# Turning the keys of a two-layer hybrid encoder: block transposes on VectorE and short-run stores in place of TensorE transposes

## The chip, the cores and the metric

The kernel runs on one core of one Trainium2 chip, as one program. The metric is the device time of that program in microseconds (us). TensorE is PE in the profile, its weight loads PEld, VectorE DVE, ScalarE ACT, GpSimd POOL and SyncE SP.

## The reference, cut to what matters

Two layers, each a mixer and a feed-forward block over 16 meta tokens and 1024 tokens (L = 1040) of width 1024. In the mixer, four heads of 128 run a gated delta rule forwards and backwards over the tokens in chunks:

```python
proj = h @ w_in
qkv, z, b_raw, a_raw, sc_b, sc_c, sc_h = jnp.split(proj, idx, axis=-1)
qkv = jax.nn.silu(depthwise_conv_centred(qkv, conv_qkv_w))
q, k, v = jnp.split(qkv, 3, axis=-1)
q, k = l2norm(q), l2norm(k)              # per head
...
M = jnp.where(strict, jnp.einsum('bnhid,bnhjd->bnhij', kb, k) * decay_mat, 0.0)
u = triangular_solve(M + I, vb); w = triangular_solve(M + I, kb * exp(G))
attn = jnp.einsum('bnhid,bnhjd->bnhij', q, k) * decay_mat
...
S = S * gl_c + jnp.einsum('bhcd,bhce->bhde', kd_c, v_new)   # in the scan over chunks
```

The last line is why the keys are needed twice: with the head's channels on partitions for the products of keys and queries, and with the tokens on partitions for the update of the state S.

## The kernel before, in words

**Layout.** Activations lie transposed, channels on partitions and 1040 tokens along the row. `KTt` (128 x 4 heads x 1040) is the normalised keys, `QT` the queries. The scan works on nine chunks: the 16 meta tokens, then eight of 128.

**Projections.** `dense` multiplies eight 128 x 128 weight tiles, split into a high and a low part, with a row of tokens in chunks of 348, 346 and 346 (in layer 1's z tiles two of 512): 24 matmuls a chunk, lines 174 to 176, into one of three accumulator banks ("acc"). Weights come by SP's queue, are split on ScalarE (line 129) and VectorE (line 130). A chunk is evicted by VectorE, line 325 in most tiles, into a row buffer (`trow`, three of them); then the bank is free. The tiles come in the order keys (4), queries (4), v (4), then z and short-convolution tiles mixed, z first.

**Side work.** After each chunk `dense` takes one entry from each of three lists (`jobs`, `jobs2`, `jobs3`). Entries are, among others, `k_out`, `chunk_p` (products of keys, lines 478 to 490), `chunk_a` (products of keys and queries, line 514; for the meta chunk with a load of "dt", lines 522 and 523), `v_store` (PE transposes of v, lines 736 and 747, the copy "vm", line 740, eviction and stores, 748 and 749), and the steps of `invert` (lines 582 to 622). This is the order in the source only: a list scheduler at build time sets the order of each engine's instructions from their dependencies, their priorities and the buffers that they wait for. On the chip every engine takes its list in order.

**The inversion.** `substitute(0)` and `substitute(1)`, one for each direction, are 31 pairs of VectorE steps each (lines 555 and 557), every pair on the result of the last; behind each come two block transposes of 128 x 1024 (lines 566 and 567), four ScalarE copies (line 569) and the chain of small matmuls of `invert`. `subs["end"]` is the last step issued.

**Keys to tokens.** `k_out(c)`, called for nine chunks from the fourth tile on: four PE transposes, one a head, into the single "a" bank (line 453), one eviction by ScalarE into a buffer "kt" (line 455), one store on ScalarE's queue of whole 2 KB rows into `vkd` in HBM (line 456). The scan reads it from there as K.

**Buffers that are shared.** `t2k` hands out 128 x 512 buffers of one tag, ck2, five in number: kt, the vm copy, r4 and rows of `query_lengths` (lines 645 to 657), dt and the chunks' qk all take from it. The "a" bank is one, banks "b" and "f" are two each. DMAs on POOL's queue are issued one by one by GpSimd.

Of the kernel before, what the change touches and what calls it, by code (L numbers as in the profile page):

```python
# [10 lines left out]
AF = mybir.ActivationFunctionType  # L11
# [7 lines left out]
H = 4  # L19
# [22 lines left out]
def trunk(ctx: ExitStack, tc: tile.TileContext, xT, w_in, w_ba, w_out, w_gu, w_dn,  # L42
          par_d, alog_d, dtb_d, cst_d, eye_d, out):
    nc = tc.nc
# [16 lines left out]
    def t2k(tag):  # L61
        return sb.tile([128, 4, 128], F32, tag="ck2", bufs=5, name=nm(tag))
# [7 lines left out]
    def pa():  # L70
        return bank("a")
# [26 lines left out]
    act = nc.scalar.activation  # L98
# [5 lines left out]
    adma = nc.scalar.dma_start  # L104
# [204 lines left out]
    for l in range(DEPTH):  # L309
# [23 lines left out]
        def trow():  # L333
            return row(Y[1], F32, 3)
# [109 lines left out]
                qdma(bc, rnd[r + h].partition_broadcast(128))  # L444
                tt(out=dst[:, h, :], in0=dst[:, h, :], in1=bc, op=ALU.mult)

        def k_out(c):

            n = 16 if c == 0 else 128
            s0 = 0 if c == 0 else 16 + 128 * (c - 1)  # L450
            ps = pa()
            for h in range(H):
                nc.tensor.transpose(ps[0:n, h * 128:(h + 1) * 128], KTt[:, h, s0:s0 + n], ident)
            kt = t2k("kt")
            act(out=kt[0:n].rearrange("p a b -> p (a b)"), in_=ps[0:n], func=AF.Copy)
            adma(vkd[c, 0:n, 1, :], kt[0:n].rearrange("p a b -> p (a b)"))


        at0 = [sb.tile([16, 4, 16], F32, tag=f"at0{d}", name=nm("at0")) for d in range(2)]
# [62 lines left out]
                adma(dt_[0:n, :, 0:n], dtd[c, d].rearrange("p (h i) -> p h i", h=4)[0:n, :, 0:n])  # L522
                tt(out=at0[d], in0=qk[0:n, :, 0:n], in1=dt_[0:n, :, 0:n], op=ALU.mult)


        B = [slice(32 * b, 32 * b + 32) for b in range(4)]

        tmp0 = []
        subs = {}
# [137 lines left out]
        for pos, i in enumerate(seq):  # L667
            hh = pos % 4
            if pos == 2:
                gate_weights()  # L670
                evp[0] = base - 60000
            t = trow()
            late = pos < (2, 1)[l]
            if l > 0 and pos == 0:
                dense_by_halves(wload(w_in[l, i], KT), x, FULL, to_row_late(t), first_banks)
            else:
                inproj(i, to_row_late(t) if late else to_row(t), pfirst if l == 0 and pos == 1 else None)
            def convolved(hi=None, lo=None, i=i, hh=hh, t=t, late=late):
                if late:
                    after(tt(out=t, in0=t, in1=rstd, op=ALU.mult), lo)  # L680
                dst = (QT if i < 4 else KTt)[:, hh, :]
                conv(t, dst, P_CV + 3 * i, hi)
                if i >= 4:
                    lengths("k", hh, dst, t)

            if l == 0 and pos == 0:
                held = convolved
                continue
            if l == 0 and pos == 1:
                pre[seq[2]] = wload(w_in[l, seq[2]], KT)  # L690
                held(*lastw)
            convolved()
            if pos == 2:
                g, negG, nGb, negE, gl, bkd = gates()
            nxt = seq[pos + 1] if pos < 7 else 8
            if nxt not in pre:
                pre[nxt] = wload(w_in[l, nxt], KT)
            if pos == 3:
                jobs.extend([None, None] + [lambda c=c: k_out(c) for c in range(9)])
                jobs2.extend([None, None, None] + [lambda c=c: chunk_p(c) for c in range(9)])  # L700

        for hh in range(4):
# [48 lines left out]
        ca = [0, 1, 8, 2, 7, 3, 6, 4, 5]  # L751
        for i in range(4):
            t = trow()
            if i == 2:
                jobs2.extend([lambda c=c: chunk_a(c) for c in ca])
            if i == 3:
                jobs3.extend([None] * (2 * l) + invert(0))
            inproj(8 + i, to_row(t))
            v = trow() if i % 2 == 0 else row(Y[1] + "f")
            conv(t, v, P_CV + 3 * (8 + i))  # L760
            act(out=v, in_=v, func=AF.Silu)
            jobs.extend([lambda i=i, v=v, c0=c0: v_store(i, v, c0) for c0 in (0, 1, 5)])
# [885 lines left out]
```

## Time and profile before

| | |
|---|---|
| runs | 2479.17, 2477.48, 2478.83 us; median 2478.83 |
| profiled execution | 2480.41 us, span 2478.6 us |
| granted TensorE clock | 0.999 |
| busy of the span | PE 99%, PEld 91%, DVE 71%, ACT 42%, POOL 7% |
| first and last key transpose (line 453) | 108.0 to 162.9 us (layer 0), 1349.8 to 1406.2 us (layer 1) |
| HBM | 254.52 MB read, 78.86 MB written |

Busy time counts an engine's instructions with overlaps merged. A group's row gives line, engine, operation, output <- input by the program's names, shape and count, then its busy time in us, the mean ns of one instruction, and the idle time ahead of them with what ended it. Since matmuls are pipelined, the mean of one is longer than the distance between two.

### The profile page before, as it was taken

The numbers are of one execution on the slowest core, as the hardware profiler recorded it, in microseconds if no ns is written. First come the engines' busy times: TensorE is split into PE (matmuls) and PEld (weight loads), VectorE is DVE, ScalarE is ACT, GpSimd is POOL, SyncE is SP. The second block draws the span as 40 slices with busy tenths as digits, with TensorE's granted clock in tenths as the row PEclk, the third lists the DMA queues.
The fourth block names the chain that finished last, engine by engine and source line by source line (L and its number), as shares of the span: only waits on it lengthen the run. The fifth ranks groups of instructions, "written<-read, shape, count | busy, mean of one in ns | idle before, by whom it ended". The sixth has DMA issues, their size and how long they took to land. (4 is left out here: it accounts for less than half of the span.)

```text
span 2478.6 us, 44860 instructions
## 1 busy us (share of the span) xinstructions
PE 2454.0 (99%) x17464; PEld 2253.9 (91%) x17464; DVE 1769.4 (71%) x3268; ACT 1053.3 (42%) x1961; POOL 171.1 (7%) x272
## 2 busy tenths in 40 slices
PE   8999999999999999999999999999999999999998
PEld 6999999999999999999999898998988888888887
DVE  5688255769987777797856883457798776777887
ACT  5675222435333333444546752324453333334454
POOL 0250101002000000000001301000110000000000
PEclk9999999999999999999999999999999999999999
DMA  4453155623432222575524532456434322228734
GB/s 133 129 177 102 62 186 168 218 86 110 149 114 96 94 82 82 200 226 164 159 88 131 171 103 70 154 170 222 126 115 147 111 93 82 81 90 271 232 105 131
DMA packets 198685, 336.34 MB, mean 136 GB/s; under 512 B 23572, under 2 KB 88920, under 8 KB 198472
## 3 DMA queue, kind: packets, MB, share of 16 engines
q1 hardware_dynamic: 174184, 295.31, 36.6%
q0 software_dynamic: 8384, 21.29, 2.8%
q10 hardware_dynamic: 15904, 16.87, 2.0%
q8 instruction: 137, 2.24, 0.4%
q14 instruction: 76, 0.62, 0.1%
HBM read 254.52 MB, written 78.86 MB: 135 GB/s over the span
## 5 line engine op out<-in xcount | busy, mean ns | idle before, releaser
L174 PE MATMUL pacc<-a,whi 128*128 128x346 f32 (+1 forms) x752 | 245.7, 330 | 7.8 <-ACT whi L129 6.0
L176 PE MATMUL pacc<-a,wlo 128*128 128x346 f32 (+1 forms) x752 | 243.9, 326 | 0.0
L174 PE MATMUL pacc<-b,whi 128*128 128x346 f32 (+2 forms) x648 | 226.2, 350 | 0.0
L176 PE MATMUL pacc<-b,wlo 128*128 128x346 f32 (+2 forms) x648 | 223.1, 346 | 0.0
L175 PE MATMUL pacc<-a,whi 128*128 128x346 f32 (+1 forms) x646 | 211.5, 328 | 0.0
L129 ACT ACTIVATE whi<-raw 128x512 fp32r<-128x512 f32 x144 | 90.4, 629 | 280.7 <-PE pacc L175 236.6
L175 PE MATMUL pacc<-b,whi 128*128 128x346 f32 (+2 forms) x559 | 193.2, 346 | 0.4 <-DVE b L954 0.4
L174 PEld LDWEIGHTS pacc<-a,whi 128*128 128x128 f32 x752 | 141.8, 189 | 12.1 <-ACT whi L129 6.0
L176 PEld LDWEIGHTS pacc<-a,wlo 128*128 128x128 f32 x752 | 142.2, 189 | 0.9 <-issue 0.4
L130 DVE TENSOR_TENSOR wlo<-raw,whi 128x512 fp32r<-128x512 f32 x144 | 99.0, 688 | 60.1 <-ACT whi L129 59.3
L174 PEld LDWEIGHTS pacc<-b,whi 128*128 128x128 f32 x648 | 121.8, 188 | 9.7 <-issue 1.5
L176 PEld LDWEIGHTS pacc<-b,wlo 128*128 128x128 f32 x648 | 121.9, 188 | 8.9 <-issue 0.8
L175 PEld LDWEIGHTS pacc<-a,whi 128*128 128x128 f32 x646 | 122.3, 189 | 3.4 <-issue 1.9
L1063 ACT ACTIVATE whi<-rw 128x512 fp32r<-128x512 f32 x98 | 61.5, 631 | 137.2 <-DVE rw L1351 43.1
L175 PEld LDWEIGHTS pacc<-b,whi 128*128 128x128 f32 x559 | 105.2, 188 | 8.1 <-issue 0.8
L1063 ACT ACTIVATE b<-rw 128x512 fp32r<-128x512 f32 x65 | 40.6, 631 | 132.9 <-PE pacc L1083 39.0
L1063 ACT ACTIVATE a<-rw 128x512 fp32r<-128x512 f32 x65 | 40.8, 629 | 111.7 <-PE pacc L1083 78.5
L484 POOL DMA_DIRECT2D ptm<-gd x35 | 19.1, 552 | 844.7 <-DVE a L325 733.7
L1064 DVE TENSOR_TENSOR wlo<-rw,whi 128x512 fp32r<-128x512 f32 x98 | 67.0, 685 | 5.6 <-ACT whi L1063 4.9
L325 DVE TENSOR_TENSOR a<-pacc,rstd 128x346 f32<-128x346 f32 (+2 forms) x59 | 32.5, 554 | 45.2 <-PE pacc L176 45.1
L325 DVE TENSOR_TENSOR b<-pacc,rstd 128x346 f32<-128x346 f32 (+1 forms) x63 | 32.1, 511 | 44.4 <-PE pacc L176 44.2
L1518 PE MATMUL pacc<-P,a 128*128 128x260 f32 x196 | 55.4, 283 | 0.0
(1050 smaller groups left out, 8103.8 us busy)
## 6 DMA issues: line engine op xcount, KB each, us to landing
raw<-in_w_in SPq DMA_DIRECT2D x112, 256.0 KB, 2.7
rw<-in_w_gu SPq DMA_DIRECT2D x96, 256.0 KB, 2.7
raw<-in_w_gu SPq DMA_DIRECT2D x96, 256.0 KB, 2.8
rec<-vkd SPq DMA_DIRECT2D x61, 256.0 KB, 3.0
b<-ad SPq DMA_DIRECT2D x55, 260.0 KB, 4.0
a<-ad SPq DMA_DIRECT2D x55, 256.0 KB, 3.6
rw<-in_w_dn SPq DMA_DIRECT2D x68, 192.0 KB, 3.5
ad<-a SPq DMA_DIRECT2D x21, 520.0 KB, 2.9
```

Source lines behind the costliest of these rows:

```text
L129: lastw[0] = act(out=hi, in_=raw[:, 0:kk, :], func=AF.Copy)
L130: lastw[1] = tt(out=lo, in0=raw[:, 0:kk, :], in1=hi.bitcast(F32), op=ALU.subtract)
L174: mm(ps[:, :n], wh, xh[:, n0:n1], start=(k == 0), stop=False)
L175: mm(ps[:, :n], wh, xl[:, n0:n1], start=False, stop=False)
L176: mm(ps[:, :n], wl, xh[:, n0:n1], start=False, stop=(k == K - 1))
L325: tt(out=t[:, n0:n1], in0=ps, in1=rstd[:, n0:n1], op=ALU.mult)
L484: qdma(gr[0:n, :, 0:n], gd[36 * d + 4 * c:36 * d + 4 * c + 4, 0:n].partition_broadcast(n))
L1063: act(out=hi, in_=src, func=AF.Copy)
L1064: tt(out=lo, in0=src, in1=hi.bitcast(F32), op=ALU.subtract)
L1518: r = mm(ps, wl[:, k, :], th[:, c0:c1], start=False, stop=e, skip_group_check=True)
```

## The change

`k_out` goes. In its place VectorE transposes the keys in blocks of 32 x 32: one instruction takes 512 tokens of one head (128 x 512), and within each of the 4 x 16 blocks rows and columns change places, but the blocks stay where they are. Four stores, one for each group of 32 partitions, then put the blocks where they belong in `vkd`: 512 runs of 32 numbers (128 bytes) each. So there are eight such instructions a layer and one for the meta tokens, with 36 stores, all on POOL's queue. They are called from `jobs2` in the v tiles instead of from `jobs` in the key tiles, and every transpose is made to come after `subs["end"]`, which is the end of `substitute(0)` there. `v`, `B` and the rest are as before.

```diff
@@ -444,16 +444,26 @@
                 qdma(bc, rnd[r + h].partition_broadcast(128))
                 tt(out=dst[:, h, :], in0=dst[:, h, :], in1=bc, op=ALU.mult)
 
-        def k_out(c):
-
-            n = 16 if c == 0 else 128
-            s0 = 0 if c == 0 else 16 + 128 * (c - 1)
-            ps = pa()
-            for h in range(H):
-                nc.tensor.transpose(ps[0:n, h * 128:(h + 1) * 128], KTt[:, h, s0:s0 + n], ident)
-            kt = t2k("kt")
-            act(out=kt[0:n].rearrange("p a b -> p (a b)"), in_=ps[0:n], func=AF.Copy)
-            adma(vkd[c, 0:n, 1, :], kt[0:n].rearrange("p a b -> p (a b)"))
+        B = [slice(32 * b, 32 * b + 32) for b in range(4)]
+
+        def to_tokens(src, half, col, q, prev=None):
+
+            s0 = 16 + 512 * half
+            kt = t2k("kt").rearrange("p a b -> p (a b)")
+            after(nc.vector.transpose(out=kt, in_=src[:, s0:s0 + 512]), prev)
+            for a in range(4):
+                q(vkd[1 + 4 * half:5 + 4 * half, :, col[0], col[1] + 32 * a:col[1] + 32 * a + 32].rearrange("c (b i) j -> i (c b) j", i=32),
+                  kt[B[a]].rearrange("i (t j) -> i t j", j=32))
+
+        def k_turn(h, half):
+
+            if half is None:
+                kt = t2k("kt")[:, :, 0:32]
+                after(nc.vector.transpose(out=kt, in_=KTt[:, :, 0:32]), subs["end"])
+                for a in range(4):
+                    qdma(vkd[0, 0:16, 1, :].rearrange("i (h a j) -> a i h j", h=4, a=4)[a], kt[32 * a:32 * a + 16])
+            else:
+                to_tokens(KTt[:, h, :], half, (1, 128 * h), qdma, subs["end"])
 
 
         at0 = [sb.tile([16, 4, 16], F32, tag=f"at0{d}", name=nm("at0")) for d in range(2)]
@@ -523,8 +533,6 @@
                 tt(out=at0[d], in0=qk[0:n, :, 0:n], in1=dt_[0:n, :, 0:n], op=ALU.mult)
 
 
-        B = [slice(32 * b, 32 * b + 32) for b in range(4)]
-
         tmp0 = []
         subs = {}
         Tm = None
@@ -696,7 +704,6 @@
             if nxt not in pre:
                 pre[nxt] = wload(w_in[l, nxt], KT)
             if pos == 3:
-                jobs.extend([None, None] + [lambda c=c: k_out(c) for c in range(9)])
                 jobs2.extend([None, None, None] + [lambda c=c: chunk_p(c) for c in range(9)])
 
         for hh in range(4):
@@ -751,6 +758,9 @@
         ca = [0, 1, 8, 2, 7, 3, 6, 4, 5]
         for i in range(4):
             t = trow()
+            if i == 0:
+                turns = [(0, None)] + [(h, half) for half in range(2) for h in range(H)]
+                jobs2.extend([lambda n=n: [k_turn(*a) for a in turns[2 * n:2 * n + 2]] for n in range(5)] + [None])
             if i == 2:
                 jobs2.extend([lambda c=c: chunk_a(c) for c in ca])
             if i == 3:
```

A line of the changed kernel is 10 higher than before from 480 to 525, 8 higher from 535 to 706 (substitute: 563 and 565; its transposes: 574 and 575; copies of r4: 654), 7 higher in `v_store` (743, 747, 754), and 10 higher behind.

The scheduler's lists move with it. VectorE around the end of `substitute(0)` of layer 0 (the step with 128x31 is its last; `b_182` is its matrix, `x_1487` that of `substitute(1)`, `pacc` an accumulator bank, `b_257` the row of the first z tile). Before:

```order
L557 TENSOR_TENSOR b_182_1478<-b_182_1478,Tm_1479 128x31
L566 STREAM_TRANSPOSE b_182_1478<-b_182_1478 128x32x32
L567 STREAM_TRANSPOSE b_182_1478<-b_182_1478 128x32x32
L555 TENSOR_TENSOR Tm_1479<-x_1486,x_1487 128x31
L602 COPY b_182_1478<-b_182_1478 32x16x32
L603 COPY b_182_1478<-b_182_1478 32x16x32
L325 TENSOR_TENSOR b_257_2245<-pacc_2258,rstd_81 128x348
L740 COPY vm_2187<-pa_2185 16x128
```

The same place in the changed kernel (`b_164` is the matrix, `kt_...` the new transposes' outputs):

```order
L565 TENSOR_TENSOR b_164_1406<-b_164_1406,Tm_1407 128x31
L462 STREAM_TRANSPOSE kt_1511<-b_38_169 128x4x32
L453 STREAM_TRANSPOSE kt_1517<-b_38_169 128x512
L453 STREAM_TRANSPOSE kt_1549<-b_38_169 128x512
L453 STREAM_TRANSPOSE kt_1555<-b_38_169 128x512
L453 STREAM_TRANSPOSE kt_1587<-b_38_169 128x512
L574 STREAM_TRANSPOSE b_164_1406<-b_164_1406 128x32x32
L575 STREAM_TRANSPOSE b_164_1406<-b_164_1406 128x32x32
L563 TENSOR_TENSOR Tm_1407<-x_1414,x_1415 128x31
```

Five transposes of keys have come in ahead of the matrix's own two, and no eviction of the z tile (line 325) follows. It stands on the same engine behind the end of `substitute(1)` (`b_248` is the first z tile's row, `at_40` the result of the meta chunk that needs a dt load):

```order
L533 TENSOR_TENSOR at_40_171<-pb_1808,dt_1816 16x64
L565 TENSOR_TENSOR x_1415<-x_1415,Tm_1407 128x2x30
L563 TENSOR_TENSOR Tm_1407<-x_1414,x_1415 128x31
L565 TENSOR_TENSOR x_1415<-x_1415,Tm_1407 128x31
L574 STREAM_TRANSPOSE b_318_2893<-x_1415 128x32x32
L575 STREAM_TRANSPOSE x_1414<-x_1415 128x32x32
L325 TENSOR_TENSOR b_248_2227<-pacc_2240,rstd_81 128x348
L325 TENSOR_TENSOR b_248_2227<-pacc_2291,rstd_81 128x346
L325 TENSOR_TENSOR b_248_2227<-pacc_2352,rstd_81 128x346
```

All three evictions of that tile have moved behind 31 pairs of steps and two transposes. In between stand the other four transposes of keys, the first vm copy and the two dt products, which were ahead of the end of `substitute(0)` before.

TensorE in layer 0 at the third chunk of the first z tile. Before, the inversion's first matmuls (line 582) and v's transposes (line 747) lie among the chunk's matmuls:

```order
L174 MATMUL pacc_2309<-a_1_72,whi_2246 128x346
L175 MATMUL pacc_2309<-a_2_73,whi_2246 128x346
L176 MATMUL pacc_2309<-a_1_72,wlo_2247 128x346
L582 MATMUL pf_1978<-b_182_1478,P_884 32x32 x32
L582 MATMUL pf_2013<-b_182_1478,P_884 32x32 x32
L747 MATMUL pa_2284<-ident,b_229_1913 128x128 x4
L174 MATMUL pacc_2309<-a_1_72,whi_2246 128x346
L175 MATMUL pacc_2309<-a_2_73,whi_2246 128x346
```

In the changed kernel the whole chain stands in one piece between the last matmul of that tile (`pacc_2352`) and the first of the second z tile (`pacc_2489`); its end and what follows:

```order
L624 MATMUL pf_2522<-b_164_1406,P_876 64x64 x8
L626 MATMUL pf_2523<-P_876,b_164_1406 64x64 x8
L626 MATMUL pf_2575<-P_876,b_164_1406 64x64 x8
L754 MATMUL pa_1750<-ident,b_178_1599 128x128 x4
L754 MATMUL pa_1801<-ident,b_178_1599 128x128 x4
L524 MATMUL pb_1887<-b_37_168,b_38_169 128x128 x4
L524 MATMUL pb_1952<-b_37_168,b_38_169 128x128 x4
L174 MATMUL pacc_2489<-a_1_72,whi_2477 128x348
```

So the small matmuls have moved from among the projections to a single place ahead of the second z tile, and the transposes of the first v tile (line 754, `b_178`) with them. Another such piece, of `turn`, `v_store` and `chunk_a`, stands behind the second z tile. Layer 1 has the same pieces one chunk of 512 later.

## The prediction

> **What bounds the kernel now.** I read the head of the page first.
>
> ```profile
> span 2478.6 us, 44860 instructions
> PE 2454.0 (99%) x17464; PEld 2253.9 (91%) x17464; DVE 1769.4 (71%) x3268; ACT 1053.3 (42%) x1961; POOL 171.1 (7%) x272
> ```
>
> Then the table by stretches of 10 us (start and end, then busy time and instructions of PE, PE's weight loads, VectorE, ScalarE, GpSimd) for the part of layer 0 that the change touches:
>
> ```profile
> 180.00:190.00 10.00, 10.00 (x66) 9.66 (x65) 8.76 (x20) 2.87 (x4) 0.00 (x0) 1.00 0.19 57
> ...
> 200.00:210.00 10.00, 10.00 (x214) 9.52 (x215) 9.53 (x24) 9.43 (x13) 0.00 (x0) 1.00 0.16 57
> 210.00:220.00 10.00, 10.00 (x215) 9.48 (x208) 9.52 (x23) 7.66 (x13) 1.14 (x1) 1.00 0.47 155
> ```
>
> TensorE works without a gap, so any PE time removed is gained and any PE wait is lost in full, and nothing later can give it back. But VectorE (9.53 and 9.52 of 10) has no room between 200 and 220 us: TensorE stays fed only because VectorE's work is well interleaved there. That is the point on which I decide.
>
> **What is removed.** Per layer 36 PE transposes and nine evictions on ScalarE. From the groups of PE and ACT between 100 and 170 us:
>
> ```profile
> L453 PE MATMUL pa<-ident,b 128*128 128x128 f32 x32 | 4.8, 274 | 0.0
> L455 ACT ACTIVATE kt<-pa 128x512 f32<-128x512 f32 x8 | 4.7, 585 | 2.9 <-PE pa L453 2.5 <-ACT ptm L487 0.4
> ```
>
> Transposes overlap, so their busy time, not their count times 274 ns, is the saving: 4.8/32 x 36 = 5.4 us a layer, 10.8 in all. If nothing else happened, the profiled execution of 2480.4 us (its span is 2478.6) would become 2469.6.
>
> **What is added on VectorE.** The trace has no 128x512 block transpose, but has ones of twice the size.
>
> ```profile
> L545 DVE STREAM_TRANSPOSE b<-b x1: 2093/2093/2093, 151.5 to 151.5; 128x1024 f32<-128x1024 f32 x1
> ```
>
> Half of 2.09 is 1.05 us; the meta one, a quarter of that, 0.3. So eight and one are 8.7 us a layer. They are bound to the end of substitute(0), and there the listed order matters more than their length. Before, VectorE ran thus (one row from further ahead, for its length; then from the end of substitute(0) to behind that of substitute(1); columns: start, duration, and in brackets the idle time ahead and what ended it):
>
> ```profile
> 166.48 0.41 DVE L646 COPY r<-pf 128x260 f32<-128x260 f32 x1
> ...
> 197.02 0.19 DVE L557 TENSOR_TENSOR b<-b,Tm 128x31 f32<-128x31 f32 x1
> 197.25 2.08 DVE L566 STREAM_TRANSPOSE b<-b 128x1024 f32<-128x1024 f32 x1
> ...
> 201.08 0.19 DVE L555 TENSOR_TENSOR Tm<-x,x 128x31 f32<-128x31 f32 x1
> ...
> 202.00 0.52 DVE L325 TENSOR_TENSOR b<-pacc,rstd 128x348 f32<-128x348 f32 x1
> ...
> 206.61 0.21 DVE L555 TENSOR_TENSOR Tm<-x,x 128x60 f32<-128x60 f32 x1
> ...
> 207.28 0.52 DVE L325 TENSOR_TENSOR b<-pacc,rstd 128x346 f32<-128x346 f32 x1
> ...
> 215.74 0.51 DVE L325 TENSOR_TENSOR b<-pacc,rstd 128x346 f32<-128x346 f32 x1
> ...
> 217.63 1.24 DVE L557 TENSOR_TENSOR x<-x,Tm 128x252 f32<-128x252 f32 x1
> ...
> 223.92 0.52 DVE L325 TENSOR_TENSOR b<-pacc,rstd 128x348 f32<-128x348 f32 x1 [1.39 <-PE pacc L176]
> ...
> 230.19 0.52 DVE L325 TENSOR_TENSOR b<-pacc,rstd 128x346 f32<-128x346 f32 x1 [1.18 <-PE pacc L176]
> ...
> 235.03 0.69 DVE L130 TENSOR_TENSOR wlo<-raw,whi 128x512 fp32r<-128x512 f32 x1 [1.02 <-ACT whi L129]
> ...
> 236.87 2.03 DVE L567 STREAM_TRANSPOSE x<-x 128x1024 f32<-128x1024 f32 x1
> ...
> 241.06 1.02 DVE L604 MEMSET b<- 32x512 f32 x2 [0.16 <-issue]
> ```
>
> The first z tile's three chunks were evicted (the first three L325) at 202.00, 207.28 and 215.74, in the middle of substitute(1). In the changed order no L325 stands between the end of substitute(0) and the end of substitute(1): all three come behind it, in layer 0 behind the next two 128x1024 transposes too. VectorE takes its instructions in order and there are three accumulator banks, so the fourth chunk, the next z tile's first, cannot start until then. The reason in the program: nine "kt" buffers now fight for the five slots of ck2, each held until its four stores have landed; the vm copy and the meta chunk's two dt loads take slots from the same five, so they move towards the end of substitute(1); v's stores come behind them; v's row buffer comes free late; and the first z tile is evicted into that buffer.
>
> **Layer 0, summed.** T is the end of substitute(0), 197.2 before. I put it at 195 (estimate: part of the 5.4 us that PE is ahead; the L325s among its steps wait for PE). Behind T on VectorE, from the rows above and these of the groups from 190 to 245 us:
>
> ```profile
> L130 DVE TENSOR_TENSOR wlo<-raw,whi 128x512 fp32r<-128x512 f32 x6 | 4.1, 687 | 1.0 <-ACT whi L129 1.0
> L602 DVE COPY b<-b 32x512 f32<-32x512 f32 x4 | 1.6, 411 | 0.0
> L604 DVE MEMSET b<- 32x512 f32 x3 | 1.5, 485 | 0.3 <-issue 0.2
> L740 DVE COPY vm<-pa 16x128 f32<-16x128 f32 x2 | 0.5, 270 | 0.0
> ```
>
> and these of the DMA issues (KB each, us from issue to landing):
>
> ```profile
> vkd<-vm SPq DMA_DIRECT2D x8, 8.0 KB, 1.6
> dt<-dtd ACTq DMA_DIRECT2D x3, 4.0 KB, 2.5
> vkd<-b ACTq DMA_DIRECT2D x4, 256.0 KB, 2.5
> ```
>
> - meta and four kt transposes: 0.3 + 4 x 1.05 = 4.5
> - the two 128x1024 transposes of direction 0: 201.08 - 197.25 = 3.8
> - two L130 (1.3), four L602/L603 (1.6), one memset (0.5), a fifth kt (1.05), the first pair of steps (0.4): 4.9
> - the other 30 pairs of substitute(1): 236.87 - 206.61 = 30.3 before, less four L325, three L130 and a vm copy inside (3.8), 3.6 us of waiting (the brackets) and the excess of the stretched step at 217.63 (0.8): 22.1
> - r4 copy 0.4 (as L646), two memsets 1.0, three kt 3.15, vm 0.25, two L523 0.4 (smaller than vm's copy): 5.2
> - the L523s wait for loads that wait for vm's store: vm store 1.6, load 2.5, less the steps between: about 1.5, and again about 1.0 for the second load, whose slot the first gives: 2.5
> - the two of direction 1: 241.06 - 236.87 = 4.2
>
> Sum 47.2: the first z chunk is evicted at 242.2, done at 242.7. v's second store, issued about 6 us behind vm's copy and landing in 2.5, is in time at about 239. PE then has the second z tile to do, 72 matmuls at 0.16, and behind that a knot of moved groups (turn, two v_store, five chunk_a) in one piece. PE's timeline at that place before, and two of its groups from 198 to 240 us:
>
> ```profile
> 238.30 0.32 PE L176 MATMUL pacc<-a,wlo 128*128 128x346 f32 x1
> 238.46 0.32 PE L174 MATMUL pacc<-a,whi 128*128 128x348 f32 x1
> ```
>
> ```profile
> L514 PE MATMUL pb<-b,b 128*128 128x128 f32 x24 | 3.3, 275 | 0.0
> L747 PE MATMUL pa<-ident,b3f 128*128 128x128 f32 x8 | 1.4, 280 | 0.0
> ```
>
> Those 72 are 11.4 us: 254.1. The knot is 5 x 0.55 + 4 x 0.7 + 0.6 = 6.1 us for PE alone and up to 10 if every step waits for the single "a" bank's eviction; I take 7.2, so 261.3. At this place (the first short-conv tile begins) before stood at 238.46: **+22.8**. About 1.1 us of v_store groups are left for later: **+23.9**. PE does the whole of invert(0) inside its wait, 15 us of work that lay between matmuls before, so the idle time to be seen is nearer 30 us than 45.
>
> **Layer 1.** z tiles have two chunks of 512 there, so PE runs one chunk further before it stops, and L325 stands ahead of the two large transposes. VectorE at the end of substitute(0), and PE where it goes on with the first short-conv tile's second chunk:
>
> ```profile
> 1438.88 0.18 DVE L557 TENSOR_TENSOR a<-a,Tm 128x31 f32<-128x31 f32 x1
> ```
>
> ```profile
> 1479.04 0.60 PE L747 MATMUL pa<-ident,a3f 128*128 128x128 f32 x4
> ...
> 1480.65 0.42 PE L174 MATMUL pacc<-b,whi 128*128 128x346 f32 x1
> ```
>
> T is about 1437 (1439.1 less 2). The same terms without the large pair (4.2) and one dt load (1.2): 41.8, L325 at 1478.8, PE on at 1479.4; one chunk of 512 (24 x 0.16 x 512/346) and the next tile's first (24 x 0.16) are 9.3: 1488.7; the knot 7.2: 1495.9. Before went on there at 1480.65: **+15.3**.
>
> 2480.4 + 23.9 + 15.3 = 2519.6. The three timed runs have a median 1.6 below the profiled one: 2518.0. Hops between engines that the sum holds at zero can only add; I forecast **2520**. PE's 10.8 us are inside it: what is gained ahead of T is waited away.
>
> **What only the new kernel has: the stores.** Each is 512 runs of 128 bytes from GpSimd, 36 a layer. The nearest rows (ns min/median/max of an issue, and us to landing for the last):
>
> ```profile
> L484 POOL DMA_DIRECT2D ptm<-gd x35: 532/543/673, 87.0 to 1376.2; - x35
> ...
> L651 POOL DMA_DIRECT2D rows<-rnd x8: 497/508/517, 169.4 to 1414.8; - x8
> ...
> L499 POOL DMA_DIRECT2D m0d<-P x3: 531/533/536, 120.3 to 1362.0; - x3
> ...
> DMA to landing us min/median/max: 4.1/4.7/5.4
> ```
>
> One run (L651) costs 0.51 us of POOL, 128 runs (L484) 0.54: nearly flat. So a store is between 0.55 (flat) and 4 x 0.54 = 2.2 us (in proportion to runs); I take 0.6, the nearer row. Scattered small runs (L499) landed in at most 5.4 us. The vm copy waits for the 24th store and stands at T + 34.5: at 0.6 that store has landed by T + 1.4 + 24 x 0.6 + 5.4 = T + 21, in time. The point from which it decides is (34.5 - 6.8)/24 = 1.15 us a store. The Trainium skill ("DMA: Bandwidth & Descriptors", "Anatomy of one DMA — SWDGE (gpsimd) path") holds that many descriptors can be emitted before the extra cost shows; the flat rows agree up to 128 runs, no run of this kernel shows 512, and by it the sum stays at 2520.
>
> **Rivals.**
> *The stores are slow on POOL* (2.2 us each, or landing times that add up). vm then waits to T + 1.4 + 52.8 + 2.5 = T + 56.7, 22 us behind T + 34.5; the same in layer 1: 2520 + 44 = 2564. For: nothing here has 512 runs. Against: the flat rows. 0.20.
>
> *PE is not held, the kernel is faster.* Place: VectorE between T and the first L325 of the z tile. For no loss in layer 0 that L325 must come 24 us earlier, so T at 171 instead of 195: only if sub(0)'s steps were done almost without the work among them, and VectorE is busy 8.8 of 10 us there already (the stretch from 180 us). If the scheduled order did not bind and z were evicted as before, only the 10.8 us less 2 to 4 us of displaced work would show: 2478.8 - 8 = 2471. 0.07.
>
> *The change comes out even*, the stall being worth just the transposes: 0.01.
>
> *The wait is shorter:* vm's and dt's waits vanish and the knot costs PE's 6.1 alone, T 3 us earlier in both layers: 2520 - 2 x 5.5 = 2509; or T without any gain and knots of 10: 2520 + 2 x 5 = 2530. These are the forecast's own range.
>
> **How the numbers follow.** Forecast 0.72 (2505 to 2535), slow stores 0.20 (2535 to 2570), the rest below. The range runs from 2500 to 2566. A measurement of this kernel can tell about 0.2%, 5 us, from no change. Faster 0.07, same 0.02, slower 0.91.
>
> **What would show it.** Right: TensorE idle some 30 us at about 200 to 243 us and, less, at 1446 to 1479, its wait ended by VectorE's L325 of the z tile; no L325 between the two substitutions; then a second, short thin place ten us later; everything else of the kernel as long as before; kt block transposes of about 1.05 us and POOL stores of about 0.6. Slow stores show as POOL DMA rows of over 1.2 us, and VectorE waiting at the sixth to eighth kt or the vm copy for landings. If PE is full from 200 to 260 us, the whole argument is wrong.

## The result, and the profile after

Timed in turn on one chip, the kernel before took 2479.0 us (median of four, 2477.48 to 2480.96) and **the changed one 2535.8 us** (median of four, 2534.42 to 2537.96): a ratio of 1.0227, 95% interval 1.0213 to 1.024. The forecast was 2520, slower by about 40 us; it is slower by 57. The profiled execution of the changed kernel took 2536.39 us.

The head of its page, and the row of granted TensorE clock over 40 slices of the span:

```profile
span 2534.6 us, 44840 instructions
PE 2474.8 (98%) x17392; PEld 2273.4 (90%) x17392; DVE 1781.2 (70%) x3286; ACT 1041.9 (41%) x1941; POOL 219.9 (9%) x344
PEclk9997999999999999999999979999999999999999
```

Two numbers of the head split the loss. The span has grown by 56.0 us. TensorE's idle time, span less busy, was 2478.6 - 2454.0 = 24.6 us and is 59.8: 35.2 more. Its busy time has grown by 20.8 us although 72 transposes are gone. That second part is not in the forecast at all, and the row of the clock says where to look: two thin slices, one in each layer.

Stretches of the stall in layer 0, and their counterpart in layer 1 (busy time and instructions of PE, weight loads, VectorE, ScalarE, GpSimd; then the granted clock):

```profile
200.00:210.00 10.00, 2.75 (x74) 2.35 (x72) 9.74 (x18) 6.10 (x8) 10.00 (x16) 0.81 0.64 136
210.00:220.00 10.00, 9.88 (x271) 9.82 (x272) 9.21 (x26) 4.77 (x9) 8.19 (x15) 0.50 0.37 58
220.00:230.00 10.00, 10.00 (x114) 10.00 (x113) 7.67 (x20) 4.14 (x7) 0.00 (x0) 0.50 0.01 2
230.00:240.00 10.00, 2.73 (x13) 1.74 (x11) 5.81 (x17) 1.78 (x3) 6.62 (x11) 0.50 0.47 74
240.00:250.00 10.00, 8.19 (x45) 8.00 (x46) 7.45 (x13) 5.51 (x6) 3.28 (x6) 0.81 0.41 99
...
1480.00:1490.00 10.00, 8.66 (x266) 8.33 (x265) 9.15 (x28) 6.22 (x11) 8.80 (x14) 0.64 0.57 97
1490.00:1500.00 10.00, 10.00 (x114) 10.00 (x113) 7.50 (x19) 3.98 (x7) 1.02 (x2) 0.50 0.01 2
1500.00:1510.00 10.00, 4.70 (x26) 3.71 (x24) 6.92 (x20) 2.55 (x5) 5.42 (x9) 0.50 0.29 50
1510.00:1520.00 10.00, 6.79 (x22) 5.63 (x22) 5.92 (x9) 1.06 (x1) 6.69 (x11) 0.50 0.57 111
```

A reader who looks only at busy time would see TensorE full from 210 to 230 us. TensorE's timeline and the clock tell otherwise: between 220 and 230 us it is the inversion's small matmuls alone, at half clock, with no projection among them. Before, the small matmuls lay among projections there, at clock 1.00:

```profile
220.00:230.00 10.00, 10.00 (x100) 9.31 (x97) 7.11 (x18) 2.98 (x5) 0.00 (x0) 1.00 0.26 87
```

VectorE on the path of layer 0, from the end of `substitute(0)` to the first z evictions:

```profile
197.97 0.19 DVE L565 TENSOR_TENSOR b<-b,Tm 128x31 f32<-128x31 f32 x1
198.20 0.31 DVE L462 STREAM_TRANSPOSE kt<-b 128x128 f32<-128x128 f32 x1
198.43 2.45 DVE L453 STREAM_TRANSPOSE kt<-b 128x512 f32<-128x512 f32 x4
...
230.74 0.48 DVE L612 MEMSET b<- 32x512 f32 x1 [2.42 <-PE pf L626]
...
237.28 0.21 DVE L533 TENSOR_TENSOR at<-pb,dt 16x64 f32<-16x64 f32 x1 [1.83 <-DMA dt<-dtd]
...
240.32 0.21 DVE L533 TENSOR_TENSOR at<-pb,dt 16x64 f32<-16x64 f32 x1 [1.51 <-DMA dt<-dtd]
240.92 0.19 DVE L565 TENSOR_TENSOR x<-x,Tm 128x31 f32<-128x31 f32 x1
...
244.82 1.37 DVE L325 TENSOR_TENSOR b<-pacc,rstd 128x348 f32<-128x348 f32 x3
```

The three evictions of the z tile stand in one row at 244.82, behind everything. The first of them was at 202.00 before. The same in layer 1, where two long waits (3.72 and 3.94 us) stand ahead of them:

```profile
1469.20 0.19 DVE L565 TENSOR_TENSOR a<-a,Tm 128x31 f32<-128x31 f32 x1
...
1501.84 1.02 DVE L612 MEMSET a<- 32x512 f32 x2 [3.72 <-PE pf L626]
...
1510.88 0.19 DVE L565 TENSOR_TENSOR x<-x,Tm 128x31 f32<-128x31 f32 x1
1515.01 1.29 DVE L325 TENSOR_TENSOR a<-pacc,rstd 128x512 f32<-128x512 f32 x2 [3.94 <-DMA vkd<-a]
```

On TensorE, the places where it goes on, where the knot of `turn`, `v_store` and `chunk_a` begins and where the first short-conv tile goes on, in layer 0 and in layer 1:

```profile
245.40 0.43 PE L174 MATMUL pacc<-a,whi 128*128 128x348 f32 x1 [1.23 <-DVE b L325]
...
257.08 0.25 PE L664 MATMUL pa<-ident,rows 36*128 36x36 f32 x1
...
266.04 0.40 PE L174 MATMUL pacc<-a,whi 128*128 128x348 f32 x1
...
1515.76 0.79 PE L174 MATMUL pacc<-b,whi 128*128 128x512 f32 x1 [3.21 <-DVE a L325]
...
1527.80 0.25 PE L664 MATMUL pa<-ident,rows 36*128 36x36 f32 x1
...
1539.05 0.43 PE L174 MATMUL pacc<-b,whi 128*128 128x346 f32 x1
```

The place at 266.04 was at 238.46 before, the one at 1539.05 at 1480.65. And the new stores (ns min/median/max of an issue, then us to landing):

```profile
L455 POOL DMA_DIRECT2D vkd<-kt x64: 651/651/853, 200.8 to 1517.9; - x64
...
DMA to landing us min/median/max: 2.3/3.0/6.4
```

### The profile page after: what moved, and what is told of

The parts are those of the page before. It is cut to its first block, busy times and chain, and to the rows that moved or that the text cites. A ratio compares the mean times of both kernels' runs of the same rounds, so it can differ in the third digit from the quotient of the medians.

```text
span 2534.6 us, 44840 instructions
## 1 busy us (share of the span) xinstructions
PE 2474.8 (98%) x17392; PEld 2273.4 (90%) x17392; DVE 1781.2 (70%) x3286; ACT 1041.9 (41%) x1941; POOL 219.9 (9%) x344
## 5 line engine op out<-in xcount | busy, mean ns | idle before, releaser
L174 PEld LDWEIGHTS pacc<-b,whi 128*128 128x128 f32 x648 | 122.3, 189 | 16.5 <-DVE a L325 4.7
L325 DVE TENSOR_TENSOR a<-pacc,rstd 128x346 f32<-128x346 f32 (+2 forms) x59 | 32.4, 554 | 46.4 <-PE pacc L176 38.6
L325 DVE TENSOR_TENSOR b<-pacc,rstd 128x346 f32<-128x346 f32 (+1 forms) x63 | 31.9, 514 | 46.9 <-PE pacc L176 44.7
L866 DVE TENSOR_TENSOR rec<-rec 128x512 f32<-128x512 f32 x32 | 22.7, 708 | 47.2 <-DMA rec<-dtd 28.7
```

The lines of the kernel that those rows point to most:

```text
L174: mm(ps[:, :n], wh, xh[:, n0:n1], start=(k == 0), stop=False)
L325: tt(out=t[:, n0:n1], in0=ps, in1=rstd[:, n0:n1], op=ALU.mult)
```

## The experiments

My theory was that the order decides: the turns, held back to the end of `substitute(0)` and taking slots that vm, dt and v need, push the z tile's evictions behind `substitute(1)`. The rivals were the number of stores, VectorE's added time, and the place in the list of jobs without the binding. Where a run is compared with the kernel before "eviction by eviction", the same evictions (lines 325 and 779) of both traces are set against each other; two numbers give how much later they are, in all, behind the disturbed part of layer 0 and behind that of layer 1, in the profiled execution. Runs are called e1 to e11. The changed kernel has +28.7 and +56.2 there, so layer 1 adds 27.5.

### The binding without the transposes on VectorE

The kernel before, with its TensorE transposes and long stores, but with `k_out` at the changed kernel's place and its evictions bound to the end of `substitute(0)`:

```diff
-                jobs.extend([None, None] + [lambda c=c: k_out(c) for c in range(9)])
...
+            if i == 0:
+                jobs2.extend([lambda n=n: [k_out(c) for c in range(9)[2 * n:2 * n + 2]] for n in range(5)] + [None])
...
-            act(out=kt[0:n].rearrange("p a b -> p (a b)"), in_=ps[0:n], func=AF.Copy)
+            after(act(out=kt[0:n].rearrange("p a b -> p (a b)"), in_=ps[0:n], func=AF.Copy), subs["end"])
```

> Edit: the kernel before, TensorE transposes and whole-row stores on ScalarE's queue, but its nine k_out moved to the place in the v tiles where the change issues its transposes, with the eviction bound to the end of substitute(0). No block transpose, no short-run store. The order has the first z tile's evictions behind substitute(1) here too, with about 32 us of VectorE work from the end of substitute(0) to them against 46.6 measured in the changed kernel. Theory A: 2500 to 2520 us. Theories B and C: neither their stores nor their VectorE work is here, 2477 to 2485 us.

Measured (e3): 2511.52 us against 2478.85, ratio 1.0128 (1.0115 to 1.0142), as expected; eviction by eviction +19.6 and +25.7 (the profiled execution was the fastest of four, 2505.46). The stretches show the same picture as the changed kernel, with no block transpose and no short run in it:

```profile
200.00:210.00 10.00, 5.90 (x145) 5.02 (x139) 8.92 (x27) 7.29 (x11) 0.00 (x0) 0.74 0.35 118
210.00:220.00 10.00, 9.76 (x170) 8.17 (x169) 7.31 (x18) 5.33 (x9) 6.30 (x12) 0.50 0.31 106
220.00:230.00 10.00, 10.00 (x75) 8.97 (x74) 5.64 (x19) 4.04 (x7) 0.00 (x0) 0.50 0.22 75
```

The same without the binding, that is, the first two pieces of that diff alone:

> Edit: the kernel before with its TensorE transposes and whole-row stores, k_out issued where the change issues its own, bound to nothing (e3 without the binding). The order keeps evictions and inversion interleaved. Theory A: the place in the source alone costs little and the binding is what costs, 2475 to 2485 us. Rival: it is the place in the list of jobs, not the binding, that makes e3 slow, 2500 us or more.

Measured (e7): 2481.83 us against 2479.33, ratio 1.0013 (1.0004 to 1.0022); +1.7 and +0.3. So the place in the list costs 2.5 us, and the binding at that place 30 more: about half of the loss of 57 comes with neither VectorE's transposes nor the short stores. By the evictions it is more of layer 0 (19.6 of 28.7) than of layer 1 (6.1 of 27.5). What is held in this run is the "a" bank with a buffer behind it, in the changed kernel the buffers alone. That the five buffers carry the hold there is read from the program and the listed order; no run gave `t2k` a sixth.

### The changed kernel without the binding, and with the turns early

```diff
-            after(nc.vector.transpose(out=kt, in_=src[:, s0:s0 + 512]), prev)
+            after(nc.vector.transpose(out=kt, in_=src[:, s0:s0 + 512]), None)
```

(and the same for the meta transpose):

> Edit: the changed kernel with the binding of each block transpose to the end of substitute(0) left out; place in the source, buffers and stores as in the change. The order now has the transposes among the evictions ahead of substitute(0), and the first z tile's evictions behind 52 of 62 steps of substitute(0), not behind substitute(1). Theory A: the loss shrinks to what is left of the wait, 2480 to 2505 us. Theory B: stores unchanged, 2525 to 2540 us. Theory C: the added VectorE work is unchanged and in a fuller stretch, 2525 us or more.

Measured (e2): 2495.09 us, ratio 1.0072 (1.0058 to 1.0085); +13.3 and +14.2. 16 us of the 57 are left. They are still a wait for the z tile's evictions, in layer 0 this one of TensorE:

```profile
210.50 0.63 PE L174 MATMUL pacc<-a,whi 128*128 128x348 f32 x1 [10.96 <-DVE b L325]
```

Unbound turns, too, push these evictions back at this place, from 202.00 to 210 us, but not behind the whole of `substitute(1)`.

Then also unbound, and put where `k_out` stood before (`jobs` at `pos == 3`, one turn a job):

```diff
+                turns = [(0, None)] + [(h, half) for half in range(2) for h in range(H)]
+                jobs.extend([None, None] + [lambda a=a: k_turn(*a) for a in turns])
```

> Edit: block transposes and short-run stores issued where the kernel before issued its k_out (jobs, from the fourth tile on), bound to nothing. VectorE is 7.6 to 9.9 of 10 us busy there. The order has the first z tile's evictions behind 43 of 62 steps of substitute(0) in a piece, and the inversion interleaved. Theory A: a smaller wait, 2470 to 2490 us. Theory B: 2525 us or more. Theory C: 2490 us or more.

Measured (e6): 2492.27 us, ratio 1.0052 (1.0038 to 1.0066); +6.3 and +11.2, a little above what I expected of my theory and inside the range of the rival, VectorE's added work in a full stretch. Its trace shows the same kind of stall one tile earlier: in layer 0 three evictions (line 325) stand in one row at 194.07, TensorE waits 6.99 us for them, and the clock is 0.51 from 190 to 200 us. Whether the order or VectorE's added time puts them there is not separated. Taking the binding away does not make the change a gain, nor does the old place.

### The stores

One store for each block transpose instead of four, in long runs. K lies in memory in the wrong order then; this part of the computation is not the reference's.

```diff
-            for a in range(4):
-                q(vkd[1 + 4 * half:5 + 4 * half, :, col[0], col[1] + 32 * a:col[1] + 32 * a + 32].rearrange("c (b i) j -> i (c b) j", i=32),
-                  kt[B[a]].rearrange("i (t j) -> i t j", j=32))
+            q(vkd[1 + 4 * half:5 + 4 * half, :, col[0], col[1]:col[1] + 128].rearrange("c p e -> p c e"), kt.rearrange("p (c e) -> p c e", c=4))
```

> Edit: the changed kernel with one store of long runs for each block transpose in place of four of short runs (8 and 4 for the meta chunk instead of 36 a layer). The blocks land untransposed among themselves, so K in memory is not the one that the scan needs: only the time is read. The order has the first z tile's evictions about 25 of 62 steps into substitute(1), some 22 us behind the end of substitute(0) against 46.6. Theory A: 2480 to 2500 us, since slots come free sooner and the eviction comes sooner. Theory B: the same gain, 2475 to 2485 us, by cheaper stores; which of the two is told by the stores' own rows (issue and landing) and by the other runs. Theory C: 2525 us or more.

Measured (e4): 2510.91 us, ratio 1.0122 (1.0105 to 1.0138); +20.8 and +31.6. It lies between my ranges, which ended at 2500 for two of the theories and began at 2525 for the third. Then the four short stores as they are, on SP's queue instead of GpSimd's (`dma` in place of `qdma` in `k_turn`):

> Edit: the changed kernel with its 36 stores a layer on SP's queue in place of GpSimd's; place, binding, buffers and runs as in the change. The order has the first z tile's evictions 25 of 62 steps into substitute(1) (as e4), and the inversion in three pieces instead of one. Theory A (place and binding; the stores only by holding the five buffers longer or shorter): the same loss as e4 and e3, 2500 to 2515 us. Theory B (it is GpSimd's queue that is dear): most of the loss gone, 2485 us or less.

Measured (e9): 2507.94 us, ratio 1.0118 (1.0104 to 1.0132); +21.7 and +29.5. Four short stores on SP cost no more than one long one on GpSimd; so the runs of 128 bytes are not the price by themselves. Both edits bring the loss from 57 to about 30 us, near that of the binding alone (e3). By the evictions most of the other 25 us or so lies in layer 1, which adds 27.5 us in the changed kernel, 10.8 with one store and 7.8 with SP's queue. These 25 us need both, the short stores on GpSimd and the bound place: the same 36 stores a layer on the same queue cost 9 us where they are late and in one lump (e1, below), and nothing where they are late and spread out (e5). Both edits also move the listed order: the first z tile's evictions then stand inside `substitute(1)` (at 221.94 and 225.66 in the two traces) instead of behind it. What part of the 25 us is the queue and what part that order is not separated.

### Turns behind everything that they displace

First, the turns behind `substitute(1)`, bound to its end; the edit also adds a memset of the `rows` buffer on GpSimd in each layer.

```diff
-            if i == 0:
-                turns = [(0, None)] + [(h, half) for half in range(2) for h in range(H)]
-                jobs2.extend([lambda n=n: [k_turn(*a) for a in turns[2 * n:2 * n + 2]] for n in range(5)] + [None])
...
             if j == 0:
                 substitute(1)
+                turns = [(0, None)] + [(h, half) for half in range(2) for h in range(H)]
+                jobs2.extend([lambda a=a: k_turn(*a) for a in turns])
```

> Edit: the same nine block transposes and 36 stores on GpSimd's queue, but issued one a chunk after substitute(1) and bound to its end, when the vm copies and dt loads have had their buffers. One small memset of the rows buffer on GpSimd is added. Theory A (the loss is the place: kt buffers held until their stores land push vm, dt, v's stores and so the first z tile's eviction behind substitute(1), and TensorE waits): the wait is gone and the removed TensorE transposes remain, 2466 to 2475 us. Theory B (the short-run stores themselves are dear, on GpSimd or in landing): 36 of them are still there, so 2500 us or more. Theory C (VectorE's 5.5 us a layer of added work in a stage where it is full): 2479 to 2495 us.

Measured (e1): 2487.56 us, ratio 1.0035 (1.0023 to 1.0048); +5.2 and +7.5. The stall at 200 us is gone, as I held, but I expected a gain; the time lies in the range of the third theory, VectorE's added work. GpSimd's and VectorE's timelines show what came in its place:

```profile
242.11 12.86 POOL L455 DMA_DIRECT2D vkd<-kt  x20
254.98 2.46 POOL L775 TENSOR_TENSOR b<-b,rstd 128x1040 f32<-128x1040 f32 x1
```

```profile
261.57 1.33 DVE L779 TENSOR_TENSOR b<-pacc,b 128x348 f32<-128x348 f32 x3
```

A product on GpSimd (line 775), which the first short-conv tile's evictions (line 779) need, stands behind twenty stores of 0.65 us. It ends at 257.44; ahead of the evictions VectorE's list then has two weight splits (line 130), which wait 4.85 and 1.16 us for ScalarE, and a block transpose, so the product is not all that holds them. Three evictions come in one lump again, TensorE does the second inversion in one piece, and the clock falls:

```profile
260.00:270.00 10.00, 9.15 (x317) 8.64 (x311) 2.57 (x5) 6.19 (x11) 5.10 (x8) 0.76 0.52 122
270.00:280.00 10.00, 10.00 (x84) 9.88 (x83) 2.14 (x2) 4.12 (x6) 0.00 (x0) 0.56 0.01 2
```

To test that, the same with the stores on SP's queue:

> Edit: e1 with the stores on SP's queue. In e1's trace GpSimd's product of the first short-convolution tile stood behind 20 stores of 0.65 us, and the evictions behind that product, and the second inversion came in one lump that ran at half clock. If that is why e1 was slower than before, 2466 to 2474 us. If the block transposes behind substitute(1) are themselves in the way (Theory C), 2482 to 2492 us as e1.

Measured (e10): 2478.57 us (ten runs, 2474.88 to 2480.65) against 2478.43, ratio 1.0001 (0.9992 to 1.001). The time lies in neither of my ranges, but the 9 us went with the queue. The listed order moved with it: the three evictions come one by one, at 257.05, 258.56 and 261.12. TensorE is full at 1.00 in the two stretches where it was not (the profiled execution is the fastest of the ten):

```profile
260.00:270.00 10.00, 10.00 (x66) 9.74 (x66) 4.86 (x6) 3.06 (x4) 0.00 (x0) 1.00 0.50 132
270.00:280.00 10.00, 10.00 (x153) 9.48 (x152) 2.86 (x6) 2.71 (x5) 2.83 (x1) 1.00 0.31 107
```

But it is not the gain that I expected, and what takes that away here was not followed. Second, one turn for each chunk from the tile `j == 3` on, each bound to that chunk's own eviction, so that no eviction can fall behind a turn; stores on GpSimd as in the change, and the memset as above:

```diff
-                tt(out=t[:, n0:n1], in0=ps, in1=rstd[:, n0:n1], op=ALU.mult)
+                lastev[0] = tt(out=t[:, n0:n1], in0=ps, in1=rstd[:, n0:n1], op=ALU.mult)
...
-                to_tokens(KTt[:, h, :], half, (1, 128 * h), qdma, subs["end"])
+                to_tokens(KTt[:, h, :], half, (1, 128 * h), qdma, lastev[0])
...
+            if j == 3:
+                turns = [(0, None)] + [(h, half) for half in range(2) for h in range(H)]
+                jobs2.extend([lambda a=a: k_turn(*a) for a in turns])
```

(line 781's eviction sets `lastev` likewise, the meta transpose is bound likewise, and the turns at `i == 0` are gone.)

> Edit: the nine block transposes and 36 short-run stores a layer as in the change, but one after each chunk of the late tiles (from the tile behind which invert(1) begins), each bound to the eviction of that chunk's own bank; the memset of the rows buffer as in e1. The order now keeps both inversions interleaved with the projections, with no piece of them in one lump. Theory A (place and what it drags behind it, the lump of small matmuls at half clock included): TensorE never waits and 5.4 us a layer of its transposes are gone, 2466 to 2472 us. Theory B (short-run stores are dear): 2480 us or more. Theory C (VectorE's added 5.5 us a layer): VectorE is about a third busy there, so 2466 to 2472 us as with A.

Measured (e5): **2471.25 us** (six runs, 2469.81 to 2472.81) against 2479.33, ratio 0.9967 (0.9955 to 0.9979): faster than both kernels; -3.5 and -5.4 by evictions. The head of its page:

```profile
span 2471.0 us, 44810 instructions
PE 2445.7 (99%) x17392; PEld 2248.6 (91%) x17392; DVE 1783.0 (72%) x3286; ACT 1041.0 (42%) x1941; POOL 218.0 (9%) x346
```

Idle time of TensorE 25.3 us, as before the change (24.6); busy time 8.3 less. This is the same work as in the changed kernel, 18 block transposes and 72 stores on GpSimd, some 64 us cheaper. The same with stores on SP:

> Edit: e5 with the stores on SP's queue. Nothing of e5 waited for GpSimd's issue, so no difference from e5 is expected beyond 0.1%: 2468 to 2474 us. If the issue on GpSimd still cost e5 something, 2460 to 2467 us.

Measured (e11): 2475.73 us (eleven runs, 2471.84 to 2479.64), ratio 0.9992 (0.9983 to 1.0001), 4 us worse than on GpSimd's queue and in neither of my ranges. With the turns out of the way GpSimd's queue does no harm. Why SP's is a little worse there was not pursued.

### The clock

The kernel before, with blocks of back-to-back float32 matmuls on a constant ahead of its work: 160 of 128x128, 900 of 32x32, 160 of 128x128, 400 of 64x64, 160 of 128x128.

```diff
+    psx = psp.tile([128, 512], F32, tag="a", bufs=1, name="psx")
+    for k, n in ((128, 160), (32, 900), (128, 160), (64, 400), (128, 160)):
+        for i in range(n):
+            nc.tensor.matmul(psx[0:k, 0:k], ones[0:k, 0:k], ones[0:k, 0:k], start=True, stop=True)
```

> Edit: the kernel before with a block of extra matmuls at its start, on a tile of ones, back to back on TensorE, nothing between them: 160 of 128x128x128, 900 of 32x32x32, 160 large, 400 of 64x64x64, 160 large. It only reads the granted clock; the span is longer by the block. Theory A (small matmuls alone do not hold the full clock, as the stretches after 1482 us of the changed kernel suggest): the clock falls to 0.50 some microseconds into the small blocks, though TensorE never idles, and rises again in the large ones; 32x32 start about every 28 ns instead of 19. Rival (only idle time lowers the clock): 1.00 throughout behind the first microseconds.

Measured (e8): one run, 2716.8 us. The trace has two records for each of these matmuls (1800 for the 900), and the counts are of records. Its stretches of 4 us: the end of the first block, the beginning and end of the 32x32 matmuls, the return with the second block, and one from the 64x64 block:

```profile
36.00:40.00 4.00, 4.00 (x46) 3.88 (x45) 0.00 (x0) 0.00 (x0) 0.00 (x0) 1.00 0.00 0
40.00:44.00 4.00, 4.00 (x132) 4.00 (x130) 0.00 (x0) 0.00 (x0) 0.00 (x0) 1.00 0.01 4
44.00:48.00 4.00, 4.00 (x83) 4.00 (x80) 0.00 (x0) 0.00 (x0) 0.00 (x0) 0.52 0.02 4
...
128.00:132.00 4.00, 4.00 (x79) 4.00 (x78) 0.00 (x0) 0.00 (x0) 0.00 (x0) 0.50 0.00 0
132.00:136.00 4.00, 4.00 (x29) 3.94 (x28) 0.00 (x0) 0.00 (x0) 0.00 (x0) 0.50 0.01 4
136.00:140.00 4.00, 4.00 (x37) 4.00 (x36) 0.00 (x0) 0.00 (x0) 0.00 (x0) 0.96 0.00 0
176.00:180.00 4.00, 4.00 (x73) 4.00 (x70) 0.00 (x0) 0.00 (x0) 0.00 (x0) 1.00 0.00 0
```

TensorE is busy 4.00 of 4 in each of these stretches, and the clock still falls to 0.50 within about 4 us of 32x32 matmuls (132 of them in 4 us, then 79) and stays there until wide ones come. A record of the 32x32 block starts every 30 ns at the full clock and every 51 at half, not 19 and 28 as I had it. The 64x64 block, for which my expectation also had a fall, holds 1.00 (its stretch from 176 to 180 us is the last row).

## Why the prediction was right, and where its size was not

**What bounds the kernel.** Right. TensorE had no slack and VectorE no room at 200 us; both showed. "Nothing later can give it back" is true of idle time, but not of lateness: in e1 the evictions are 15.9 us late at the one that stood at 269.25 before and 5.2 at the one at 311.00, because the inversion's matmuls, done early in one piece, are then missing among the projections.

**The order.** Right in each of its signs: no L325 between the substitutions, TensorE's wait ended by VectorE's L325, a second thin place behind the second z tile. The cause was argued from the listed order. The changed kernel with the binding alone taken away (e2) loses 16 us instead of 57, e3 against e7 shows the binding without the change, and e5 shows that the same work in another place gains.

**T, the end of `substitute(0)`.** This step failed. The forecast let T come 2.2 us earlier in layer 0 (195) and 2 in layer 1; it came at 197.97 + 0.19 = 198.2, which is 1.0 later than before. In layer 1 it came at 1469.4, that is 1439.1 plus the 28.7 carried over plus 1.6. Error +3.2 and +3.6. TensorE's saving did not last until T. Between 155 and 160 us TensorE waits 1.11 us for ScalarE's half of a weight split (line 129) and 1.36 for VectorE's (line 130), and from 160 to 165 its clock is 0.50. It does 33 matmuls from 155 to 165 us, where it did 70 before; at 0.16 us each that is about 6 us, as much as the 5.4 saved in the layer. The forecast had no wait and no fall of the clock there. e5 has waits in the same place too (1.0, 0.9 and 0.6 us), at clock 1.00. Of the 10.8 us that the forecast took off TensorE, e5 shows 8.3 in busy time.

**From T to the first z eviction.** In sum right in layer 0: 244.82 - 198.2 = 46.6 against 47.2. But by two errors that cancel. The kt transposes were priced at 1.05 us each and cost 0.67, overlapping a little (four in 2.45): -3.6 for the eight and the meta one. And a wait stands there that no term held: 2.42 us at the memset of line 612, for the last matmuls of the inversion. Within the stall the forecast put the whole inversion beside VectorE's work and held it at full clock; at 0.50 it took longer, and that this made it late is argued from these rows. One 64x64 matmul took 221 ns before; these are its groups from 198 to 240 us before, and to 246 after, with the gap ahead of the chain's larger part in the rows behind, in layer 0 and in layer 1:

```profile
L616 PE MATMUL pf<-b,P 64*64 64x64 f32 x64 | 4.6, 221 | 0.0
```

```profile
L624 PE MATMUL pf<-b,P 64*64 64x64 f32 x64 | 7.6, 314 | 0.0
```

```profile
210.12 1.75 PE L590 MATMUL pf<-b,P 32*32 32x32 f32 x58 [6.11 <-ACT b L593]
...
1481.61 1.10 PE L590 MATMUL pf<-a,P 32*32 32x32 f32 x58 [1.33 <-ACT a L593]
```

The 64x64 matmul took 314 ns in the stall. The dt waits were 1.83 and 1.51 against 1.5 and 1.0. In layer 1 the same sum came to 45.6 against 41.8: 3.72 us at line 612, and 3.94 for v's second store. That store was issued at 1508.8 and landed some 6 us later, not the 2.5 that was taken for it. Row loads and kt stores were issued on GpSimd in these microseconds; that they delayed it is not tested.

**TensorE from there to the knot.** 257.08 - 245.40 = 11.7 against 11.4 in layer 0. In layer 1 1527.80 - 1515.76 = 12.0 against 9.3 (the forecast's own factors give 9.5): the clock was 0.56 from 1516 to 1521 us, so the chunk of 512 took 7.8 us (1515.76 to 1523.55) where its 24 matmuls at the forecast's rate are 5.7. The clock that was taken as 1 is most of this term's error.

**The knot.** 7.2 us were taken between bounds of 6.1 and 10. It took 266.04 - 257.08 = 9.0 and 1539.05 - 1527.80 = 11.3. The clock was mostly 1.00 there; the excess is hops between ScalarE, VectorE and TensorE on the single bank, and in layer 1 a wait for an activation and 32 matmuls of the second inversion in the same piece:

```profile
1538.43 0.69 PE L590 MATMUL pb<-a,P 32*32 32x32 f32 x32 [2.16 <-ACT qk L527]
```

Layer 0: 3.2 - 0.6 + 0.1 + 0.3 + 1.8 = +4.8, which is the 28.7 measured against 23.9. Layer 1: 3.6 + 3.8 + 0.1 + 2.7 + 4.1 = 14.3 at the place compared, of which some 2 us are given back behind it: 27.5 measured against 15.3. So the mechanism was right, the size short by 17 us, most of it in layer 1. "Hops between engines that the sum holds at zero can only add" names the direction; the sum should have given them a price.

**The idle time.** "Nearer 30 us than 45" in layer 0 was wrong as a reading: 7.3 + 0.1 + 7.3 + 1.8 = 16.5 us are idle from 200 to 250. The rest of the stall is filled with matmuls, most of them at half clock. e5 has the same number of matmuls; against it TensorE is busy 29.1 us longer in the changed kernel (2474.8 against 2445.7) and idle 34.5 longer. How much the clock itself costs was not isolated; no run held it up through the stall.

**The stores.** The choice of 0.6 us was right (0.651), the rival of 2.2 wrong. By the Trainium skill ("DMA: Bandwidth & Descriptors", "Anatomy of one DMA — SWDGE (gpsimd) path") the sum was to stay where it was, and the rows now agree up to 512 runs: a store of 512 runs issues in 0.65 us. But "in time" was only half the matter: e4 and e9 show that fewer stores, or the same on another queue, take 25 us off the bound version, most of it in layer 1. The forecast looked at the issue of the 24th store alone.

**The rivals.** "TensorE is not held, the kernel is faster" gave 2471 if the z evictions stay where they were. That is not what the change did, but it is what e5 did by another order: 2471.25.

## What to carry to other kernels

In a kernel whose order is listed ahead, what a moved block costs is set by what it pushes back on an in-order engine and in a shared set of buffers, far more than by its own time: here the same 18 transposes and 72 stores cost 57 us at one place and gained 8 at another. Bind such work to something behind the evictions that it could displace, and look on each queue it uses for a computation that stands behind it. When a stall is forecast, price the work inside and just behind it at the clock that TensorE is granted there, not at that of the full stretches.

## What the runs showed of the hardware

- Matmuls of 32x32 back to back, with TensorE never idle, brought the granted clock to 0.50 within about 4 us (132, then 79 of them in 4 us); 64x64 kept 1.00, and within 4 us of 128x128 matmuls it was back at 0.96. The Trainium skill ("TensorE: Matmul & The Clock Gate", "What's actually happening") has the gate drop the clock after an idle window of about 3.4 us. The changed kernel's fall at 206 us in layer 0 has such a gap, 6.11 us up to 210.12, though the clock falls some 2.3 us into it (0.64 from 206 to 207 us). Its fall in layer 1 comes at 1483 us (0.93 in the microsecond before, 0.50 from there on) in the middle of the 32x32 matmuls, with no gap ahead of it from 1470 us on that is longer than the 1.33 us at 1481.61. In the run with the blocks there is no gap at all. So an idle window is not the only thing that goes ahead of a fall.
- Between 220 and 230 us of the changed kernel the clock stayed at 0.50 through 64x64 matmuls with TensorE at 10.00 of 10. Alone, after a warm block, the same size kept 1.00. So a size that holds the clock did not bring it back here; why was not tested.
- A 128x512 block transpose of float32 took 0.67 us, a third of the 2.09 us of the 128x1024 row and not half. That row's transposes go over views of 128x32x32; whether the view makes the difference was not tried.
